# Pair 6 of the output projection by seven products in two of four groups, with its step orders rearranged

## The chip, the core and the metric

The kernel runs on one core of a Trainium2 chip. The core has TensorE (matrix products into PSUM, eight banks of 512 fp32 columns), VectorE, ScalarE and GpSimd (POOL) beside it, and queues that start DMA transfers; SyncE (SP) issues most loads. Each engine executes its own instructions in order and meets the others at semaphores. The metric is the time of one execution in microseconds (us), lower being better; runs are given as a median with the lowest and highest.

## The reference

One layer of a streaming encoder on 256 tokens of width 2048, in float32: a norm, a gated linear attention with four heads in chunks of 64 tokens, its output projection added to the residual, a norm, an MLP with squared ReLU added to the residual, and a final norm. Cut to what matters here:

```python
def _gla_mixer(h, w_in, w_gate_up, b_gate, o_norm, w_out):
    proj = h @ w_in                       # q, k, v, r, g_low
    ...
    _, o = lax.scan(step, s0, (qc, k_dec, vc, chunk_decay))
    o = o * lax.rsqrt(jnp.mean(o * o, axis=-1, keepdims=True) + EPS) * o_norm
    ...
    return (o * jax.nn.silu(r)) @ w_out   # (256, 2048) @ (2048, 2048): the output projection

h = h + _gla_mixer(_rmsnorm(h, gla_norm[j]), ...)
h = h + _sq_relu_mlp(_rmsnorm(h, mlp_norm[i]), mlp_w_up[i], mlp_w_down[i])
return _rmsnorm(h, final_norm)
```

The change lies in the output projection, `(o * silu(r)) @ w_out`.

## The kernel before, in words

**Precision by three products.** Every matrix product is made in a reduced fp32 format (`F32R`): each factor is split into a hi part (a rounded copy, made on ScalarE, L118) and a lo part (the rest, made on VectorE: L131 for weights), and a product is hi x hi + hi x lo + lo x hi, three matmuls on TensorE, each with 128 x 128 stationary values and 256 moving columns. Weights come from memory into a `raw` tile (six of them) and are split into `hi` and `lo` tiles (five of each). SP's loads wait for a free raw tile, the splits for free hi and lo tiles.

**The output projection** runs over four groups of 512 output columns (`out_group(g, ...)`, g from 0 to 3). In each group eight steps run over the contraction, a step being a pair of 128 rows (pair kp of `w_out`, 256 rows); the order of the pairs is the tuple `ORDER`. Both halves of the tokens have one PSUM bank each, started with the residual `h` (`begin_out`, called at step 3 for the next group). At the end of a group `h` is written back from the banks.

A step is done in one of two ways. *Plainly*: two halves of tokens x two halves of rows x two blocks of 256 columns = 8 block products, 24 matmuls. *By sums*: a 2 x 2 block product with seven products (Winograd's form of Strassen's method), 21 matmuls. It needs sums of the weight blocks and sums of the activation blocks (*forms*, eight blocks S3, S2, S1, S4, A12, A11, A22, A21 of 128 columns). For the weights:

- the first sum is made by the load: POOL issues a DMA that adds block 1 of the first half onto block 0 in the raw tile (`accum_op`, L742), behind the two loads of 256 KB each (L741) that replace the plain step's one of 512 KB (L744);
- blocks 1 to 3 are cast and split (768 columns), and the first three products (9 matmuls) run;
- `weight_sums` (L602, L603) makes the others in place on VectorE; they are cast (two casts of 512 columns, L118) and split (L771) into a second pair of hi and lo tiles;
- the last four products (12 matmuls) run behind the next step's products (`pending`).

Two of the seven products' targets are the token banks; the others go to the two banks p16 and p57, one pair for all groups. Behind the group's last step by sums ScalarE copies p16 and p57 out (L777, L778), VectorE combines them (L779 to L782) and adds them to `h` with the token banks (L785).

**The turns.** A product needs its activations with the contraction in the partitions. `turn` transposes four blocks of rows of 128 columns on TensorE (L625) into two spare banks and splits them into hi and lo on ScalarE (L638) and VectorE (L639); for a pair that goes by sums `turn_pair` makes the eight forms instead (copies L614, sums L615, cast L616, split L617). The pairs 0, 1 and 7 (`FORMED`) go by sums in all four groups, twelve steps of 32. The last quarter of the attention's output, pairs 6 and 7 among it, is turned in group 0 behind step 1. In the groups 1 to 3 the finished rows of `h` of the group before are turned behind step 1 for the MLP's up projection, which follows.

**What sets the order.** The program is written in the order above, and a planner lays out each engine's queue from it by its own estimates of times; where the text says `tc.issue_after`, an instruction is kept behind another on its engine. `then_mm` keeps blocks of matmuls in the written order (inside one block they may change places). Casts of weights keep their order among each other; copies, sums and turns may come between.

Of the kernel before, what the change touches and what calls it, by code (L numbers as in the profile page):

```python
# [33 lines left out]
T = 256  # L34
# [12 lines left out]
G = 1024  # L47
# [12 lines left out]
OFF = 48  # L60
# [8 lines left out]
def tile_gla_mlp(ctx, tc, x, xt, cols, w_vg, w_in, w_gate, w_out, w_up, w_down, final_norm, out):  # L69
# [19 lines left out]
    def aux_bank():  # L89
        aux_free.rotate(-1)  # L90
        return psum_bank(aux_free[-1], "aux")
# [151 lines left out]
    g2 = lambda kt: colt[:, KT + kt : KT + kt + 1]  # L243
# [88 lines left out]
    h = const.tile([P, NT, D], F32, name="h")  # L332
# [249 lines left out]
    oth = otl = None  # L582
# [13 lines left out]
    def form_sums(f, tt):  # L596
        tt(f[:, S3], f[:, A21], f[:, A11], ALU.subtract)
        tt(f[:, S2 : S1 + 1], f[:, A22 : A22 + 1].to_broadcast([P, 2, P]), f[:, 0::7], ALU.add)
        tt(f[:, S4], f[:, A12], f[:, S2], ALU.subtract)
# [2 lines left out]
        nc.vector.tensor_tensor(u[:, 2], u[:, 0], u[:, 2], op=ALU.subtract)  # L602
        return nc.vector.tensor_tensor(u[:, 1::2], u[:, 1::2], u[:, 2:3].to_broadcast([P, 2, T]), op=ALU.subtract)  # L603

    FORMED = (0, 1, 7)
    in_forms = lambda a: a.rearrange("p (f s) -> p f s", f=8)
    raw_forms = [in_forms(some[:, 4:6].rearrange("p a b -> p (a b)")), in_forms(mid.tile([P, G], F32, tag="db", name="form"))]

    def turn_pair(kp, bank, gain, to):

        raw_form = raw_forms[kp == 1]
        for i in range(2):
            s = bank[:, i * T : (i + 1) * T].rearrange("p (t s) -> p t s", t=NT)
            nc.scalar.activation(raw_form[:, A12 + 1 - i :: 2], s, AF.Copy, scale=gain(2 * kp + i))  # L614
        form_sums(raw_form, lambda o, x, y, op: nc.vector.tensor_tensor(o, x, y, op=op))  # L615
        nc.scalar.copy(to[0], raw_form)  # L616
        nc.vector.tensor_tensor(to[1], raw_form, to[0].bitcast(F32), op=ALU.subtract)  # L617

    def turn(src, row, gain, q, forms_of=None, banks=None):

        bs = banks or [aux_bank(), aux_bank()]
        for i in range(4):
            kt, b, o = 4 * q + i, bs[i // 2], i % 2 * T
            for t in range(NT):
                newest[0] = nc.tensor.matmul(  # L625
                    b[:, o + t * P : o + (t + 1) * P], src[:, t, kt * P : (kt + 1) * P], ident, is_transpose=True,
                    start=i % 2 == t == 0, stop=i % 2 == t == 1, skip_group_check=True,
                ).ins
        for kp in (2 * q, 2 * q + 1):
            if forms_of and kp in FORMED:  # L630
                turn_pair(kp, bs[kp - 2 * q], gain, forms_of(kp))
                continue
            for kt in (2 * kp, 2 * kp + 1):
                i = kt - 4 * q
                b, o = bs[i // 2], i % 2 * T
                s = b[:, o : o + T].rearrange("p (t s) -> p t s", t=NT)
                dh, dl = row(kt)
                nc.scalar.activation(dh, s, AF.Copy, scale=gain(kt))  # L638
                nc.vector.scalar_tensor_tensor(dl, s, gain(kt), dh.bitcast(F32), op0=ALU.mult, op1=ALU.subtract)  # L639
# [5 lines left out]
    oth, otl = (big.tile([P, KT * T + 192], F32R, tag="B", name="ot" + i) for i in "hl")  # L645
# [4 lines left out]
    def forms_o(kp):  # L650
        if kp < 2:
            return [of_pairs[:, kp, i] for i in range(2)]
        return [a[:, OFF : OFF + G].rearrange("p (f s) -> p f s", f=8) for a in (oth, otl)]

    def place_o(kt):

# [5 lines left out]
    def row_o(kt, t):  # L662
        if kt // 2 in FORMED:
            return [a[:, (A11, A21)[t] - kt % 2] for a in forms_o(kt // 2)]
        o, d = place_o(kt)
        return [a[:, o + t * d : o + t * d + P] for a in (oth, otl)]
# [12 lines left out]
    def begin_out(g):  # L679

        for t in range(NT):
            out_banks[g, t] = bank = psum_bank(out_ids[2 * (g % 2) + t])
            nc.scalar.copy(bank, h[:, t, g * GT : (g + 1) * GT])

    def spare_out(g):
        return [psum_bank(out_ids[2 * (1 - g % 2) + t], "aux") for t in range(NT)]

    side.extend([nothing] * 2 + [lambda: (
        turn(on, turned_o, gain_o, 0, forms_o),
        turn(on, turned_o, gain_o, 1, forms_o, [psum_bank(i, "aux") for i in r_banks[4:]]),  # L690
    )])
    side.extend([nothing] * 7 + [lambda: begin_out(0)])
# [7 lines left out]
    GROUPS = D // GT  # L700
# [86 lines left out]
    def ssq_h(g):  # L787
        for t in range(NT):
            sq = tmp.tile([P, GT], F32, tag="t512", name="sq", bufs=1)
            nc.scalar.activation(sq, h[:, t, g * GT : (g + 1) * GT], AF.Square, accum_out=hs[:, t, g : g + 1])  # L790

    ORDER = (3, 0, 2, 1, 4, 7, 5, 6)
    newest[0] = None
    ordered[0] = True
    out_group(0, ORDER, FORMED, {
        1: lambda: (turn(on, turned_o, gain_o, 2), turn(on, turned_o, gain_o, 3, forms_o, spare_out(0))),
        3: lambda: begin_out(1),
    })
    hth, htl = (big.tile([P, KT, T], F32R, tag="A" + i, name="h" + i, bufs=1) for i in "hl")
    turned_h = lambda kt: [a[:, kt, :].rearrange("p (t s) -> p t s", t=NT) for a in (hth, htl)]  # L800
    for g in range(1, GROUPS):
        out_group(g, ORDER, FORMED, {
            1: lambda: turn(h, turned_h, g2, g - 1), 4: lambda: ssq_h(g - 1),
            **({3: lambda: begin_out(g + 1)} if g + 1 < GROUPS else {}),
        })
    sums = [big.tile([P, 4, T], F32, tag="E" + i, name="sums", bufs=1) for i in "hl"]
# [444 lines left out]
    for t in range(NT):  # L1251
# [19 lines left out]
        for on_act, lo, hi in ((0, 0, 256), (1, 1280, 1536), (0, 256, 768), (1, 1536, 2048), (0, 768, 1280)):  # L1271
            s = hf[:, t, lo:hi]
# [44 lines left out]
```

## Time and profile before

| | |
|---|---|
| median of 3 runs | 1043.96 us (1043.85 to 1045.01) |
| profiled execution | 1043.57 us, its span 1041.6 us |
| granted TensorE clock, mean | 0.998 |
| output projection in the span | 286.9 to 374.5 us |
| TensorE, VectorE, ScalarE, POOL busy | 99%, 83%, 71%, 12% |

The profile is of one execution; its times run from the span's first instruction. PE is TensorE's matmuls, DVE VectorE, ACT ScalarE, SP SyncE. A row of a group of instructions names line, engine, operation, written and read tiles, shapes and count, then busy time, the mean ns of one and the idle time before it with what ended it. A row of the timeline has start, length, instruction and count, and in brackets the idle time before it with what ended it. A row of a stretch has the busy time of each engine in it, with the count of instructions, the granted clock and the share of time in which the DMA engines were busy. Matmuls overlap, so each shows 0.28 us where one begins every 0.11.

### The profile page before, as it was taken

The page shows a single profiled execution, that of the slowest core. Times are in us where ns is not written, and L with a number is a line of the kernel's source. Part 1 is how long each engine was busy: PE and PEld are TensorE (multiplying, and loading weights), DVE is VectorE, ACT ScalarE, POOL GpSimd, SP SyncE. Part 2 cuts the span into 40 slices and gives each one's busy share as a digit, 9 for nine tenths or more (in the row PEclk, how much of TensorE's full clock was granted, in tenths as well). Part 3 has the DMA queues.
Part 4 walks back from the last instruction along what each step waited for, and adds up shares of the span by engine and source line. Part 5 has one row for each costly group of instructions (what it writes and reads, how often), then busy time and mean ns, then how long its engine had stood idle before and what let it go on. Part 6 is the DMA issues. An engine that isn't in the chain of part 4 may idle for free.

```text
span 1041.6 us, 23168 instructions
## 1 busy us (share of the span) xinstructions
PE 1033.5 (99%) x9058; PEld 1033.3 (99%) x9058; DVE 865.3 (83%) x1171; ACT 736.7 (71%) x1088; POOL 119.8 (12%) x163
## 2 busy tenths in 40 slices
PE   9999999999999999999999999999999999999997
PEld 9999999999999999999999999999999999999997
DVE  5768654657499876889999999999999999999887
ACT  6785544546477665677788788778778778878685
POOL 0000000010111101111111121111111111111100
PEclk9999999999999999999999999999999999999999
DMA  9957665655667787678887888888888988888772
GB/s 340 335 167 217 191 199 143 182 145 179 190 186 208 209 262 195 178 210 228 230 248 218 239 232 225 235 240 219 245 232 225 245 230 228 232 234 221 235 239 91
DMA packets 118733, 226.79 MB, mean 218 GB/s; under 512 B 10672, under 2 KB 27184, under 8 KB 118496
## 3 DMA queue, kind: packets, MB, share of 16 engines
q1 hardware_dynamic: 100096, 207.39, 64.1%
q0 software_dynamic: 17856, 16.26, 10.4%
q8 instruction: 71, 1.16, 0.4%
q10 hardware_dynamic: 672, 1.66, 0.4%
q14 instruction: 38, 0.31, 0.1%
HBM read 223.17 MB, written 2.10 MB: 216 GB/s over the span
## 4 chain that ended last, share of the span: by engine, by line
PE 99%; issue 0%; ACT 0%; DVE 0%; POOLq 0%; POOL 0%; DVEq 0%
PE up L865 33%; PE acc L865 28%; PE acc L176 19%; PE acc L723 8%; PE acc L219 6%; PE aux L219 2%; PE aux L176 1%; PE aux L625 1%; PE aux L521 1%; PE aux L252 0%; ACT sqf L1204 0%; PE acc L422 0%; DVE hf L1276 0%; POOLq L1313 0%; POOL rf L356 0%
## 5 line engine op out<-in xcount | busy, mean ns | idle before, releaser
L118 ACT CAST hi<-raw 128x512 fp32r<-128x512 f32 (+4 forms) x634 | 512.1, 834 | 233.8 <-PE acc L176 69.1
L131 DVE TENSOR_TENSOR lo<-raw,hi 128x768 fp32r<-128x768 f32 (+3 forms) x226 | 238.0, 1057 | 97.2 <-ACT hi L118 94.4
L865 PE MATMUL acc<-hi,act 128*128 128x256 f32 x1696 | 247.7, 276 | 0.0
L865 PE MATMUL up<-hh,hi 128*128 128x256 f32 x1024 | 238.7, 276 | 0.0
L865 PE MATMUL up<-hl,hi 128*128 128x256 f32 x1024 | 238.7, 276 | 0.0
L165 DVE TENSOR_TENSOR lo<-raw,hi 128x1024 fp32r<-128x1024 f32 x160 | 194.8, 1220 | 28.1 <-ACT hi L118 26.0
L865 PEld LDWEIGHTS acc<-hi,act 128*128 128x128 f32 x1696 | 217.6, 188 | 0.0
L865 PEld LDWEIGHTS up<-hl,hi 128*128 128x128 f32 x1024 | 192.3, 188 | 0.0
L865 PEld LDWEIGHTS up<-hh,hi 128*128 128x128 f32 x1024 | 192.3, 188 | 0.0
L1075 POOL DMA_DIRECT2D raw<-in_w_down x112 | 97.3, 869 | 516.3 <-DMA raw<-in_w_down 248.2
L1135 DVE TENSOR_TENSOR lo<-raw,hi 128x1024 fp32r<-128x1024 f32 x112 | 136.5, 1219 | 1.1 <-ACT hi L118 1.1
L865 PE MATMUL up<-hh,lo 128*128 128x256 f32 x1024 | 137.0, 276 | 0.0
L865 PE MATMUL acc<-lo,act 128*128 128x256 f32 x848 | 133.8, 276 | 0.0
L865 PEld LDWEIGHTS up<-hh,lo 128*128 128x128 f32 x1024 | 125.7, 188 | 0.0
L865 PEld LDWEIGHTS acc<-lo,act 128*128 128x128 f32 x848 | 113.4, 188 | 0.0
L176 PE MATMUL acc<-hi,xA 128*128 128x256 f32 (+1 forms) x736 | 106.1, 279 | 0.0
L176 PEld LDWEIGHTS acc<-hi,xA 128*128 128x128 f32 x736 | 94.9, 189 | 0.0
L603 DVE TENSOR_TENSOR raw<-raw 128x512 f32<-128x512 f32 x124 | 85.6, 690 | 3.2
L176 PE MATMUL acc<-lo,xA 128*128 128x256 f32 (+1 forms) x368 | 61.3, 278 | 0.0
L602 DVE TENSOR_TENSOR raw<-raw 128x256 f32<-128x256 f32 x124 | 52.5, 423 | 2.9
L176 PEld LDWEIGHTS acc<-lo,xA 128*128 128x128 f32 x368 | 50.8, 188 | 0.0
L219 PE MATMUL acc<-xA,hi 128*128 128x256 f32 x288 | 49.2, 276 | 0.0
(181 smaller groups left out, 1220.4 us busy)
## 6 DMA issues: line engine op xcount, KB each, us to landing
raw<-in_w_up SPq DMA_DIRECT2D x128, 512.0 KB, 4.7
raw<-in_w_down SPq DMA_DIRECT2D x224, 256.0 KB, 4.4
raw<-in_w_in SPq DMA_DIRECT2D x80, 512.0 KB, 3.9
raw<-in_w_down POOLq DMA_DIRECT2D x112, 128.0 KB, 5.1
raw<-in_w_out SPq DMA_DIRECT2D x20, 512.0 KB, 4.7
raw<-in_w_down SPq DMA_DIRECT2D x16, 512.0 KB, 5.6
raw<-in_w_vg SPq DMA_DIRECT2D x14, 520.0 KB, 8.5
raw<-in_w_out SPq DMA_DIRECT2D x24, 256.0 KB, 3.5
```

The costliest lines, as they stand in the source:

```text
L118: last_hi[0] = nc.scalar.copy(to, raw)
L131: last_lo[0] = nc.vector.tensor_tensor(lo[:, s], raw[:, s], hi[:, s].bitcast(F32), op=ALU.subtract)
L165: last_lo[0] = nc.vector.tensor_tensor(to[1], dst, to[0].bitcast(F32), op=ALU.subtract)
L176: nc.tensor.matmul(o[:, m], x, w[:, m], start=first and c == 0, stop=last, skip_group_check=True)
L219: nc.tensor.matmul(o, u[:, i, s], m, start=kt == 0 and n == 0 and j % 2 == 0, stop=kt == KT - 1 and n == 2, skip_group_check=True,)
L521: nc.tensor.matmul(o, kab[:, k[0], c0 + c, k[1] : k[1] + P], q(qt[:, c0 + c]), start=c == 0, stop=c == 1)
L602: nc.vector.tensor_tensor(u[:, 2], u[:, 0], u[:, 2], op=ALU.subtract)
L603: return nc.vector.tensor_tensor(u[:, 1::2], u[:, 1::2], u[:, 2:3].to_broadcast([P, 2, T]), op=ALU.subtract)
L723: newest[0] = nc.tensor.matmul(bank[:, o + d : o + d + T], x, w[:, d : d + T], start=bank in sums_banks and bank.name not in begun, stop=l ...
L865: newest[0] = nc.tensor.matmul(o, x, w, start=first, stop=last, skip_group_check=True).ins
L1075: nc.gpsimd.dma_start(out=raw[:, :T], in_=src[:, 0, T:], accum_op=ALU.add)
L1135: last_lo[0] = nc.vector.tensor_tensor(to[1][:, :G], u, to[0][:, :G].bitcast(F32), op=ALU.subtract)
```

## The change

Pair 6 joins the pairs that go by sums, but only in groups 2 and 3 (fourteen steps by sums in all); in groups 0 and 1 it stays plain and reads its rows out of the forms. Its forms are made in group 0, behind step 1, where it was turned before, and lie where its rows lay. The scratch tile for forms is now chosen by the pair's parity, so pair 7 takes the one that pair 1 had. Groups 2 and 3 take the pairs in another order, 0 first and 6 and 5 last. In group 3 the turn of `h` stands behind step 3 instead of step 1.

```diff
-    FORMED = (0, 1, 7)
+    FORMED = (0, 1, 6, 7)
...
-        raw_form = raw_forms[kp == 1]
+        raw_form = raw_forms[kp % 2]
...
-        return [a[:, OFF : OFF + G].rearrange("p (f s) -> p f s", f=8) for a in (oth, otl)]
+        c = (12 * T + OFF + 128, OFF)[kp - 6]
+        return [in_forms(a[:, c : c + G]) for a in (oth, otl)]
...
-    ORDER = (3, 0, 2, 1, 4, 7, 5, 6)
+    ORDER = (3, 0, 2, 1, 4, 7, 5, 6), (0, 3, 2, 1, 7, 4, 6, 5)
+    summed = lambda g: FORMED if g > 1 else (0, 1, 7)
...
-    out_group(0, ORDER, FORMED, {
+    out_group(0, ORDER[0], summed(0), {
...
-        out_group(g, ORDER, FORMED, {
-            1: lambda: turn(h, turned_h, g2, g - 1), 4: lambda: ssq_h(g - 1),
+        out_group(g, ORDER[g > 1], summed(g), {
+            3 if g == GROUPS - 1 else 1: lambda: turn(h, turned_h, g2, g - 1), 4: lambda: ssq_h(g - 1),
```

## The prediction

> **What bounds the kernel now.** I read the page first (busy shares, the chain that ended last), then the chain in order of time, then the stretches of the four groups of the output projection.
>
> ```profile
> span 1041.6 us, 23168 instructions
> PE 1033.5 (99%) x9058; PEld 1033.3 (99%) x9058; DVE 865.3 (83%) x1171; ACT 736.7 (71%) x1088; POOL 119.8 (12%) x163
> PE 99%; issue 0%; ACT 0%; DVE 0%; POOLq 0%; POOL 0%; DVEq 0%
> ```
> ```profile
> 335.90 20.82 PE acc L723 x183
> ```
> ```profile
> core 0: us, PE busy (x) PEld busy (x) DVE busy (x) ACT busy (x) POOL busy (x), PEclk, DMA share, GB/s
> 286.90:309.40 22.50, 22.50 (x201) 22.50 (x200) 21.12 (x33) 18.07 (x29) 1.95 (x3) 1.00 0.59 176
> 309.40:331.10 21.70, 21.70 (x193) 21.70 (x192) 20.17 (x28) 16.11 (x27) 3.33 (x4) 1.00 0.76 217
> 331.10:352.80 21.70, 21.70 (x193) 21.70 (x192) 19.51 (x28) 15.74 (x26) 2.62 (x3) 1.00 0.75 214
> 352.80:374.50 21.70, 21.70 (x193) 21.70 (x192) 18.70 (x26) 15.05 (x24) 0.00 (x0) 1.00 0.73 225
> ```
>
> TensorE is the chain from end to end, and in none of the four groups (one row each) does it stand idle, at full granted clock. So a matmul less is time less, every wait of TensorE is time more, and anything else counts only where its cover runs out. One matmul is worth 20.82 / 183 = 0.114 us. A group has 5 x 24 + 3 x 21 = 183 of them and the turn's transposes. VectorE is the second: 19.5 of 21.7 us in the third group.
>
> **The matmuls.** A step by sums has 9 + 12 = 21 matmuls, a plain one 24. Pair 6 becomes a step by sums in the third and fourth group: 2 x 3 x 0.114 = 0.68 us less. Nothing else of TensorE's work changes in number: pair 6 in the first two groups reads its plain rows out of the forms, with the same 24.
>
> **What the two steps add on VectorE and ScalarE.** VectorE, a stretch of the fourth group in order of time, columns start, length, instruction:
>
> ```profile
> 354.35 0.95 DVE L131 TENSOR_TENSOR lo<-raw,hi 128x768 fp32r<-128x768 f32 x1
> 355.21 0.69 DVE L785 TENSOR_TENSOR h<-acc,some 128x512 f32<-128x512 f32 x1
> 355.82 0.42 DVE L602 TENSOR_TENSOR raw<-raw 128x256 f32<-128x256 f32 x1
> 356.27 0.69 DVE L603 TENSOR_TENSOR raw<-raw 128x512 f32<-128x512 f32 x1
> 356.88 1.22 DVE L131 TENSOR_TENSOR lo<-raw,hi 128x1024 fp32r<-128x1024 f32 x1
> 358.01 1.22 DVE L771 TENSOR_TENSOR lo<-raw,hi 128x1024 fp32r<-128x1024 f32 x1
> 359.15 0.87 DVE L639 SCALAR_TENSOR_TENSOR hl<-aux,colt,hh 128x256 fp32r<-128x256 f32 x2
> ```
>
> From start to start: 0.86 + 0.45 + 0.61 + 1.14 = 3.06 us for a step by sums, 1.13 for a plain one. So each of the two steps adds 1.93 us: the third group comes to 19.51 + 1.93 = 21.44 us in a stretch of 21.70 - 0.34 = 21.36, full, and the fourth to 20.63. The waits that VectorE has there (2.2 us of the old third group, 3.0 of the fourth) may not close up. Of the fourth's, 1.6 stand in one wait for TensorE to release a buffer, where VectorE is as far ahead as it may be (below); they are no loss. So by the worst count it falls behind by 21.44 + 2.2 - 21.36 = 2.3 us and by 20.63 + 1.4 - 21.36 = 0.7, 3.0 us. What hides that is the lead of the lo parts over their matmuls:
>
> ```profile
> 371.52 2.36 DVE L165 TENSOR_TENSOR lo<-raw,hi 128x1024 fp32r<-128x1024 f32 x2 [1.60 <-PE acc L723]
> ```
> ```profile
> 341.15 1.22 DVE L131 TENSOR_TENSOR lo<-raw,hi 128x1024 fp32r<-128x1024 f32 x1
> ```
> ```profile
> 346.47 0.39 PE L723 MATMUL acc<-lo,oth 128*128 128x256 f32 x2
> ```
>
> Pair 5 in the third group is ready at 342.37 and first read at 346.47: 4.1 us of lead, the smallest I find in these two groups. So the two steps cost nothing on VectorE, with 1.1 us to spare by the worst count; without that cover they would cost the 3.0. ScalarE casts 768 + 1024 columns instead of 1024: about 1 us a step more (a cast of 1024 is 1.05 us in L616's row below) on 15.7 of 21.7: nothing.
>
> **The forms of pair 6** are made in the first group, in the turn behind step 1, beside those of pair 7.
>
> ```profile
> 299.13 1.22 DVE L617 TENSOR_TENSOR otl<-some,oth 128x1024 fp32r<-128x1024 f32 x1
> 302.78 3.22 DVE L131 TENSOR_TENSOR lo<-raw,hi 128x1024 fp32r<-128x1024 f32 x3
> ```
> ```profile
> L616 ACT CAST oth<-some 128x1024 fp32r<-128x1024 f32 x1 | 1.0, 1046 | 0.0
> ```
> ```profile
> L615 DVE TENSOR_TENSOR some<-some 128x128 f32<-128x128 f32 (+1 forms) x6 | 2.0, 328 | 0.0
> L639 DVE SCALAR_TENSOR_TENSOR otl<-aux,colt,oth 128x256 fp32r<-128x256 f32 x10 | 4.4, 477 | 0.0
> ```
> ```profile
> 301.61 0.39 PE L723 MATMUL acc<-hi,oth 128*128 128x256 f32 x2
> 301.83 0.39 PE L723 MATMUL acc<-hi,otl 128*128 128x256 f32 x2
> ...
> 306.71 0.39 PE L723 MATMUL acc<-hi,oth 128*128 128x256 f32 x2
> ```
>
> ScalarE gets 1.05 us more; VectorE 3 x 0.33 + 1.22 less two of 0.48, 1.25 us more. Covers: pair 7's lo form ends at 300.35 and is first read at 301.83, 1.5 us; pair 6's weights end near 304.0 (the first of three) and are read from 306.71, 2.7 us. If pair 6's forms go ahead of pair 7's, 0.2 us of the first cover is left. I take 0; bounds 0 and 0.8 (1.05 + 1.25 one behind the other, less 1.5).
>
> **The wait the new order adds.** All groups share one pair of banks for the sums (p16, p57). Before, the last step by sums was pair 7, at step 5, and a plain step lay between its end and the next group. Now pair 6's second half ends the third group, and the fourth begins with pair 0 by sums, whose first products go to p16. ScalarE must copy p16 in between:
>
> ```profile
> 306.68 0.59 ACT L777 COPY some<-acc 128x512 f32<-128x512 f32 x1 [0.27 <-PE acc L723]
> ```
> ```profile
> 327.01 2.32 ACT L118 CAST hi<-raw 128x1024 fp32r<-128x1024 f32 x3 [1.95 <-PE acc L723]
> 329.24 0.58 ACT L777 COPY some<-acc 128x512 f32<-128x512 f32 x1
> ```
> ```profile
> 327.04 0.28 PE L723 MATMUL acc<-hi,oth 128*128 128x256 f32 x1
> ...
> 328.40 0.39 PE L723 MATMUL acc<-hi,oth 128*128 128x256 f32 x2
> ```
>
> In the first group the copy started 0.03 us before the 12 products were issued out (306.71), and ended at 307.27: a p16 product right behind would have waited 0.56 us. In the second, casts stood ahead: the copy ended at 329.82, 1.42 us after 328.40. So TensorE, with all that is queued behind it, waits 0.56 to 1.42 us once. Six products of pair 0 go to another bank (two of the three, 0.68 us), and within such a block the order by which instructions are issued may differ from the written one: at 301.61 the hi products of two blocks stand first. With these ahead, 0 to 0.74 remain. Bounds 0 and 1.42; I take 0.4, the middle of the second pair of ends: the casts stood ahead of the copy in the second group, and the planner has moved products in the first.
>
> The Trainium skill, "TensorE: Matmul & The Clock Gate", section "Step-by-step: what each phase is for", says that the matmuls stay in program order and only weight loads are pulled ahead. By it the chip itself would fill nothing of this wait, and if the planner doesn't either, the sum would be -0.68 + 1.42 = +0.74 at worst; no row of this trace shows a matmul waiting for ScalarE. The second group's end has no such wait: its last sums are still at step 5, and the copy there (329.82) is over 1.3 us before the third group's first product (331.1).
>
> **The turns.** In the third group the turn still stands behind step 1, now after 9 + 24 + 12 products instead of 24 + 9, so 1.4 us later; its h rows have more cover. In the fourth, h comes later: two copies of 0.58, four adds of 256 columns (0.42 as in L602's row) and two sums of 0.69 stand behind the last products, 4.2 us. The turn moves past the second half of pair 0, pair 2 and pair 1, to 78 products, 8.9 us, into the group, so some 4 us are left. It takes eight transposes on TensorE as before, four ScalarE and four VectorE copies, no DMA. Their rows are first read by the up projection's fifth step, 374.5 + 4 x 24 x 0.114 = 385.4, some 17 us behind. Both at 0. The last h hangs on pair 6's second half, one plain step (2.7 us) later than on pair 7's. What is made of it ended at 381.74 and was read at 386.29:
>
> ```profile
> 381.46 0.28 DVE L820 TENSOR_SCALAR work<-ident,r 128x128 f32<-128x128 f32 x1
> ```
> ```profile
> 386.29 0.60 PE L828 MATMUL row<-work,ones 128*128 128x128 f32 x4
> ```
> Of 4.5 us of cover 1.8 are left: nothing.
>
> **The loads.** Two more halves of 256 KB instead of one of 512, two more accumulations on POOL.
>
> ```profile
> 346.28 0.88 POOL L742 DMA_DIRECT2D raw<-in_w_out x1 [5.21 <-DVE lo L131]
> 351.15 0.88 POOL L742 DMA_DIRECT2D raw<-in_w_out x1 [3.99 <-DMA raw<-in_w_out]
> ```
> ```profile
> 362.34 0.42 DVE L602 TENSOR_TENSOR raw<-raw 128x256 f32<-128x256 f32 x1
> ```
> ```profile
> DMA to landing us min/median/max: 3.4/4.5/6.4
> ```
> Accumulations follow each other 4.9 us apart, four take 19.5 of 21.4 us; pair 7's lands by 357.6 at the slowest and its sum is made at 362.34. I take 0.
>
> **Sum:** -0.68 + 0.4 + 0 + 0 = -0.28 us. The profiled execution is 1043.57 us (span 1041.6 and 1.97 around it); it would be 1043.29. The median of the three runs, 1043.96, is 0.39 above it; predicted is 1043.7.
>
> **Rivals.** A: the wait for p16 costs its whole 1.42 and pair 7's late forms 0.8: -0.68 + 2.22 = +1.54, 1045.5; for it, the casts ahead of the copy; against, six products that could fill it. Still within 0.2%. B, slower: the accumulations of pair 7 (now right behind pair 1) and pair 6 land late, because their raw buffers come free late. The sum of weights waits at the head of VectorE's queue and holds up every lo part behind it. A delay of one accumulation, 4.9 us, eats the lead of 4.1 and leaves 0.8 at each of four places: -0.68 + 3.2 + 0.4, 1046.9. It decides once the landings slip by more than 4.1 us, or VectorE's lag does; for it, the full third group; against, 4.8 us between landing and use. C: the new plan of the queues takes waits away elsewhere: nearly nothing to take, since TensorE waits nowhere here; at most the 0.68, 1043.3.
>
> **Chances.** Forecast 0.66 (C's end in it), A 0.20, B 0.12, a gain that no row shows 0.02. A measurement of this kernel tells 0.2%, 2.1 us, from no change: faster 0.02, same 0.86, slower 0.12. The range goes from the profiled execution with the whole gain, 1043.57 - 0.68 = 1042.9, to A with half of what the slowest run, 1045.01, lies above the median: 1045.5 + 0.5 = 1046.0; B lies outside.
>
> **What would show it.** Right: 180 matmuls in the third and fourth group; one gap of TensorE under 1.5 us between them, behind it the copy of p16; VectorE near 99% in the third group, still ahead of its readers. Wrong: TensorE waiting for lo parts, for pair 7's forms near 302, or VectorE's sums of weights waiting for DMA.

## The result and the profile after

The kernel before takes 1043.99 us (median of 22 runs, 1043.49 to 1045.01), the changed one 1045.66 (22 runs, 1044.86 to 1046.36): a ratio of 1.0015, 95% interval 1.0009 to 1.0021. Forecast was 1043.7, 0.3 us under the kernel before; it became 1.7 us longer instead. That lies within the range given (1042.9 to 1046.0) and under the 0.2% that I took for the limit of a measurement, but with so many runs the sign is sure, and the sum had the other one. The profiled execution took 1045.25 us.

From the page of the changed kernel, span and TensorE:

```profile
span 1043.5 us, 23178 instructions
PE 1033.9 (99%) x9052; PEld 1033.2 (99%) x9052; DVE 868.7 (83%) x1179; ACT 736.9 (71%) x1093; POOL 121.3 (12%) x165
```

Six matmuls fewer, and yet TensorE is busy 0.4 us longer, with the same 99%. The busy share can't show what happened; the chain of waits in order of time can (start, length, line, count of matmuls). Before:

```profile
287.02 3.75 PE acc L723 x33
...
374.67 11.79 PE up L865 x104
...
975.07 3.63 PE acc L865 x32
...
1012.78 15.88 PE acc L176 x140
```

After:

```profile
287.15 3.75 PE acc L724 x33
...
362.56 12.02 PE acc L724 x102
374.57 10.38 PE up L867 x88
...
976.48 3.63 PE acc L867 x32
...
1014.18 15.88 PE acc L176 x140
```

Two lengths are read from these rows for every kernel below. The *stretch* runs from the output projection's first row to the row of 32 matmuls in the down projection: 975.07 - 287.02 = 688.05 us before, 689.33 after, +1.28. The *end* runs from the row of 140 matmuls to the end of the span: 28.8 and 29.3, +0.5. Where the projection starts differs between executions (287.0 to 288.6 in all the profiles; in the latest, e10, the chain of waits holds a load of the program's first weights until 21.6 us); here it makes 0.13. Together 1.9, which is the difference of the spans.

**In the stretch: the spacing.** Before, the up projection's first four steps take 11.79 / 104 = 0.1134 us a matmul; after, 12.02 / 102 and 10.38 / 88 are both 0.118, four per cent more. TensorE's timeline shows where that begins. Before, around the fourth group's turn (columns as in the timelines of VectorE in the prediction; the next row of two matmuls begins 0.227 us behind the last one, or 0.24):

```profile
356.56 1.04 PE L625 MATMUL aux<-ident,h 128*128 128x128 f32 x8
...
358.38 0.40 PE L723 MATMUL acc<-hi,otl 128*128 128x256 f32 x2
358.62 0.40 PE L723 MATMUL acc<-lo,oth 128*128 128x256 f32 x2
358.87 0.39 PE L723 MATMUL acc<-hi,oth 128*128 128x256 f32 x2
359.09 0.39 PE L723 MATMUL acc<-hi,otl 128*128 128x256 f32 x2
```

After the eight transposes the matmuls come 0.12 us apart, for about a dozen; from 358.87 on 0.113. The step in which this ends is pair 2's. After:

```profile
357.70 0.40 PE L724 MATMUL acc<-hi,oth 128*128 128x256 f32 x2
357.94 0.40 PE L724 MATMUL acc<-hi,otl 128*128 128x256 f32 x2
...
359.14 0.39 PE L724 MATMUL acc<-hi,oth 128*128 128x256 f32 x2
359.36 0.39 PE L724 MATMUL acc<-hi,otl 128*128 128x256 f32 x2
...
361.52 1.04 PE L625 MATMUL aux<-ident,h 128*128 128x128 f32 x8
...
362.87 0.28 PE L724 MATMUL acc<-hi,oth 128*128 128x256 f32 x1
362.99 0.28 PE L724 MATMUL acc<-hi,otl 128*128 128x256 f32 x1
...
386.55 0.28 PE L867 MATMUL up<-hl,hi 128*128 128x256 f32 x1
387.63 0.68 PE L830 MATMUL row<-work,ones 128*128 128x128 f32 x4 [0.81 <-DVE work L822]
...
391.13 0.28 PE L867 MATMUL up<-hh,hi 128*128 128x256 f32 x1
391.24 0.28 PE L867 MATMUL up<-hl,hi 128*128 128x256 f32 x1
```

The 0.12 us begin behind the moved turn and do not end: some 206 matmuls, up to 386.66, are that far apart. Only the up projection's sixth step, behind one whose weights lie differently, is back at 0.11. Pair 2, which stood behind the turn before, had gone by (from 357.70) when the turn came. Its own first dozen take 0.12 us each here too, with no turn ahead of them. So the dozen behind each turn in the trace of before does not show what a turn does, since pair 2's step follows every turn of the projection there; the experiments have to part the two.

**In the stretch: the wait.** The row product (387.63 above) waits for VectorE. The matmul after 386.55 was due at 386.66, so TensorE loses 0.97 us (the 0.81 in brackets is counted from the modelled end of the last matmul). How late its operands are is seen on ScalarE and VectorE. ScalarE before and after, the copies of the sums' banks behind the group's last step by sums:

```profile
372.49 0.58 ACT L777 COPY some<-acc 128x512 f32<-128x512 f32 x1
```
```profile
370.05 5.37 ACT L118 CAST hi<-raw 128x512 fp32r<-128x512 f32 x6 [1.25 <-DVE raw L603]
375.32 0.58 ACT L778 COPY some<-acc 128x512 f32<-128x512 f32 x1
```

VectorE, the last rows of h before, and from them to the row product's operands after:

```profile
377.07 0.68 DVE L785 TENSOR_TENSOR h<-acc,some 128x512 f32<-128x512 f32 x1
```
```profile
371.85 5.76 DVE L165 TENSOR_TENSOR lo<-raw,hi 128x1024 fp32r<-128x1024 f32 x5
...
381.88 1.28 DVE L786 TENSOR_TENSOR h<-acc,some 128x512 f32<-128x512 f32 x2
...
386.06 1.23 DVE L165 TENSOR_TENSOR lo<-raw,hi 128x1024 fp32r<-128x1024 f32 x1 [1.08 <-ACT hi L118]
387.20 0.48 DVE L822 TENSOR_SCALAR work<-ident,r 128x128 f32<-128x128 f32 x2
```

The copies begin 2.8 us later, as they should for one step later. But h is done 5.4 us later (383.16 against 377.75), for five lo parts stand in a row ahead of its adds and more between them; and the row product's operands, at 387.68 against 381.74, are 5.9 us later, for they stand behind a lo part that itself waits 1.08 us for its cast.

**What stayed quiet.** VectorE's load of the third and fourth group, by stretches (the columns are those of the stretches in the prediction):

```profile
331.10:352.60 21.50, 21.50 (x192) 21.50 (x190) 19.57 (x27) 14.19 (x26) 3.49 (x4) 1.00 0.66 198
352.60:374.50 21.90, 21.90 (x191) 21.90 (x190) 20.49 (x29) 16.63 (x28) 0.87 (x1) 1.00 0.66 197
```

TensorE waits for no lo part, no form and no weight sum. The granted clock is 1.00 in the slow stretch too. And between the third and the fourth group, TensorE and ScalarE:

```profile
352.60 0.62 PE L724 MATMUL acc<-hi,of 128*128 128x256 f32 x4
...
353.28 0.39 PE L724 MATMUL acc<-hi,oth 128*128 128x256 f32 x2
...
355.43 0.39 PE L724 MATMUL acc<-hi,of 128*128 128x256 f32 x2
355.66 0.28 PE L724 MATMUL acc<-lo,of 128*128 128x256 f32 x1
```
```profile
352.57 0.59 ACT L778 COPY some<-acc 128x512 f32<-128x512 f32 x1 [0.42 <-PE acc L724]
```

The planner put pair 0's six products to the other bank first and most of pair 3's behind them; the three to p16 come at 355.43, long after the copy (353.16).

### The profile page after: what moved, and what is told of

The parts are those of the page before. It is cut to its first block, busy times and chain, and to the rows that moved or that the text cites. A ratio compares the mean times of both kernels' runs of the same rounds, so it can differ in the third digit from the quotient of the medians.

```text
span 1043.5 us, 23178 instructions
## 1 busy us (share of the span) xinstructions
PE 1033.9 (99%) x9052; PEld 1033.2 (99%) x9052; DVE 868.7 (83%) x1179; ACT 736.9 (71%) x1093; POOL 121.3 (12%) x165
## 4 chain that ended last, share of the span: by engine, by line
PE 98%; DMA 0%; issue 0%; ACT 0%; DVE 0%; SPq 0%; POOLq 0%; POOL 0%; DVEq 0%
PE up L867 33%; PE acc L867 28%; PE acc L176 18%; PE acc L724 8%; PE acc L219 6%; PE aux L219 2%; PE aux L176 1%; PE aux L625 1%; PE aux L521 1%; DMA raw<-in_w_vg 0%; ACT hi L118 0%; ACT sqf L1206 0%; SPq L168 0%; DVE lo L165 0%; PE acc L422 0%
```

## The experiments

All differences below are against the kernel before (stretch 688.05, end 28.8), unless said otherwise.

| run | median us | ratio (95%) | stretch | end |
|---|---|---|---|---|
| the changed kernel | 1045.66 | 1.0015 (1.0009 to 1.0021) | +1.28 | 29.3 |
| e1_turn_alone | 1044.77 | 1.0008 (0.9999 to 1.0017) | +0.93 | 28.8 |
| e2_turn_shift_first | 1044.72 | 1.0008 (0.9999 to 1.0017) | +0.58 | 28.8 |
| e5_no_offset | 1047.34 | 1.0034 (1.0022 to 1.0046) | +3.27 | 28.8 |
| e7_thirteen | 1044.70 | 1.0006 (0.9996 to 1.0015) | +0.60 | 28.8 |
| e9_last_turn_later | 1044.73 | 1.0007 (0.9998 to 1.0016) | +0.34 | 29.3 |
| e6_turn_back | 1044.82 | 1.0008 (0.9998 to 1.0017) | +0.66 | 29.2 |
| e3_pair2_behind_turn | 1045.20 | 1.0012 (1.0004 to 1.0021) | +0.91 | 29.3 |
| e4_pair2_pair6_early | 1045.17 | 1.0012 (1.0003 to 1.0021) | +0.91 | 29.3 |
| e8_both_mended | 1043.64 | 0.9997 (0.9988 to 1.0006) | -0.68 | 29.2 |
| e10_loads_halved | 1044.24 | 1.0004 (0.9995 to 1.0013) | 0.00 | 29.2 |
| e11_mended_one_load | 1043.07 | 0.9991 (0.9983 to 1.0000) | -0.68 | 28.9 |

The medians of single kernels move by some tenths with the start of the projection; the stretch is read from one profile each, but where the plan of the projections is the same it repeats to 0.01 us (before and e10, e8 and e11), so it carries the verdicts. By the medians alone most of these kernels can't be told from the one before: only the changed kernel, e5, e3 and e4 have intervals clear of 1.

**The theory.** The moved turn costs about 0.9 us of spacing, since no step with the differing layout follows it; pair 6 at the group's end costs 0.97 at the row product; the six matmuls are saved as said. The rival: the slower spacing comes with the fourteen sums (VectorE and the accumulating loads busier, memory shared), and the place of the turn has no part in it.

### The turn alone, and the layout

The kernel before, with the turn of the fourth group moved and nothing else:

```diff
-            1: lambda: turn(h, turned_h, g2, g - 1), 4: lambda: ssq_h(g - 1),
+            3 if g == GROUPS - 1 else 1: lambda: turn(h, turned_h, g2, g - 1), 4: lambda: ssq_h(g - 1),
```

> The kernel before, with one edit: the fourth group's turn stands behind step 3 instead of step 1, so behind pair 2 instead of ahead of it. Theory R (rhythm): a turn leaves TensorE in a slower rhythm, one matmul of 256 columns every 0.118 us instead of 0.1134, until a step with the shifted row layout has passed (pair 2 in the projection, the fifth step of the up projection). Then some 105 + 104 matmuls between this turn and the last turn run slow: +0.9 to +1.0 us, about 1044.9, with rows 0.12 apart from near 362 to near 388 and no wait. Rival T (traffic): the slower rhythm came from DMA and VectorE traffic, which two more steps by sums brought; here it doesn't come, and the time stays within 0.2 us of before. Rival Q (queues): only waits cost; no change.

The chain, fourth group from the turn on and the up projection's first steps:

```profile
363.36 12.37 PE acc L723 x105
375.73 12.25 PE up L865 x104
```

12.25 instead of 11.79 for the same 104 matmuls, +0.93 us over the stretch, without any of the sums of pair 6. The rival falls: the place of the turn is enough.

Now the other side: the kernel before with pair 2's rows laid like all others, so that no step of the projection has the differing layout (its two rows of blocks stand 64 columns further apart than others, and their two halves of tokens 48; `place_o`). The rows behind pair 2's begin 128 columns earlier with it; pair 3, which runs ahead of the first turn, keeps its 0.113 us:

```diff
-    BOTH = (4, 5)
+    BOTH = (99,)
```

> The kernel before, with pair 2's rows laid like all others (no shift of 64 columns, no gap between the two halves of tokens). Theory R: nothing ends the slower rhythm behind the turn of the first group until the up projection's fifth step: some 33 + 3 x 183 + 183 - 33 + 104 matmuls, about 800, times 0.0045 us, less the twelve slow ones of pair 2 in each group that both have: +3.0 to +3.6 us, about 1047.3. Rival T: the layout has nothing to do with it; within 0.3 us of before.

```profile
293.43 21.56 PE acc L723 x183
```

Each group takes 21.56 instead of 20.82 for its 183, from the first group's turn on, and the first up steps 12.25 for 104: +3.27 us. So a turn starts the slow spacing that lasts, and pair 2's layout ends it. That it is these two is shown; what makes it so is not.

The third run takes e1's kernel and lays the weights of the first up step with a gap between their halves, as the fifth has them:

```diff
-                even = ((4,), (0,))[q] if m == 0 else ...
+                even = ((0, 4), (0,))[q] if m == 0 else ...
```

> The kernel before with the fourth group's turn behind step 3 (the first experiment, +0.93 us), and the up projection's first step too gets the shifted weight layout. Theory R: the slow rhythm ends in that step, some 85 matmuls early: 0.35 to 0.4 us less, +0.55. If the fifth step ends the rhythm for another reason than its layout, +0.93 stays.

```profile
375.30 11.89 PE up L865 x104
```

The up steps are back at 11.89 (0.10 over 11.79, which is some 22 matmuls still slow, nearly the whole first step), 0.35 us of the 0.93 return. So the layout may be that of weights as well as of activations.

### The row product's wait

The changed kernel with the last turn, and the row product ahead of it, one step later in the up projection:

```diff
-    ... + [nothing] * 2 + [last_turn])
+    ... + [nothing] * 4 + [last_turn])
...
-                even = ((4,), (0,))[q] if m == 0 else ...
+                even = ((5,), (0,))[q] if m == 0 else ...
```

> The changed kernel, with the last turn (the row product and the turn of the fourth group's rows) one step of the up projection later, and the step with the shifted weight layout moved along, from the fifth to the sixth. All times are from the projection's first matmul to the down projection, against the kernel before: the changed kernel is +1.28 us. If the row product's wait for VectorE (0.97) is a loss of its own, it goes, and the slow rhythm runs 24 matmuls (0.1 us) longer: +0.4. If the wait only follows from the late end of the fourth group and moves along with the row product, +1.3 stays.

The wait is gone, and the stretch falls from +1.28 to +0.34: 0.94 of the 0.97. What is left is -0.68 and the spacing, now over 24 matmuls more (102 + 128 at 0.0044 us each is 1.01): +0.33.

In the next, pair 6 goes by sums in the third group only:

```diff
-    summed = lambda g: FORMED if g > 1 else (0, 1, 7)
+    summed = lambda g: FORMED if g == 2 else (0, 1, 7)
```

> The changed kernel with pair 6 by sums in the third group alone, thirteen steps; orders and turns as in the changed kernel. The fourth group's last step by sums is then pair 7, at step 4. The row product's wait goes (0.97), three matmuls come back (0.34), the slow rhythm stays: against the kernel before +0.6 to +0.7 us between the projection's first matmul and the down projection. If the wait doesn't hang on pair 6's place at the end, +1.6.

Half the saving (-0.34), the whole spacing (+0.93), no wait: +0.59 worked out, +0.60 measured. So the wait comes with pair 6's sums in the fourth group.

Last, the changed kernel with the turn back behind step 1:

```diff
-            3 if g == GROUPS - 1 else 1: lambda: turn(h, turned_h, g2, g - 1), ...
+            1: lambda: turn(h, turned_h, g2, g - 1), ...
```

> The changed kernel with the turn of the fourth group back behind its first step, and nothing else. By the theory of the rhythm, pair 2 then stands behind the turn again and the 206 slow matmuls (0.118 us each) go: -0.99 us. But the turn would come at about 357.7 on the changed kernel's scale, and the second sum of h that it reads ends at 359.15 there: TensorE waits about 1.4 us or more once. The row product's wait of 0.97 stays. So the stretch of the projections is 1.3 to 1.8 us longer than before (the changed kernel: 1.28), the time 1045.3 to 1046. By my prediction's step, that the moved turn costs nothing in its new place and about what its h is late in the old one, the kernel would be slower than the changed one by the whole 1.4 us: 1047.

```profile
358.01 0.38 PE L625 MATMUL aux<-ident,h 128*128 128x128 f32 x2
359.52 0.88 PE L625 MATMUL aux<-ident,h 128*128 128x128 f32 x6 [1.12 <-DVE h L786]
```

The spacing is cured, and the turn waits for h once: from its first transpose to the matmul behind its last it takes 2.14 us instead of 0.79, so what follows comes 1.35 us late, and -0.68 + 1.35 = +0.67 is the +0.66 measured. That is 0.6 to 1.1 us less than I expected, because the row product's wait, which I had thought would stay, is gone: its operands are ready at 385.81, 1.6 us ahead. Pair 6's sums end the group here too; but VectorE's queue is laid out otherwise, with the adds to h (from 380.85) and the operands each ahead of a lo part that stood ahead of them in the changed kernel. So the wait of 0.97 is not pair 6's lateness alone but its lateness together with the places that the planner chose. And the move of the turn, against leaving it, cost 0.62 us in the stretch (1.28 against 0.66): what it avoided, 1.35, was less than the 0.93 and 0.97 that came with it, the second by way of the plan.

### Pair 2 behind the turn

If the theory holds, an order that leaves the turn late and puts pair 2 behind it should take the 0.93 away. Two such orders of the fourth group in the changed kernel:

```diff
-    ORDER = ..., (0, 3, 2, 1, 7, 4, 6, 5)
+    ORDER = ..., (0, 3, 2, 1, 7, 4, 6, 5), (0, 3, 1, 7, 2, 4, 6, 5)     # e3
+    ORDER = ..., (0, 3, 2, 1, 7, 4, 6, 5), (0, 3, 1, 7, 2, 6, 4, 5)     # e4
...
-        out_group(g, ORDER[g > 1], summed(g), {
+        out_group(g, ORDER[max(g - 1, 0)], summed(g), {
```

> The changed kernel, but the fourth group takes its pairs as 0, 3, 1, 7, 2, 4, 6, 5, so that pair 2 follows the turn behind step 3. The same fourteen steps by sums. Theory R: the slower rhythm ends with pair 2's first twelve matmuls: 0.9 us less than the changed kernel, and the wait of the row product for the last h (1.0 us) stays: about 1044.7. Rival T: as much traffic as in the changed kernel, the rhythm stays slow to the last turn: 1045.6.

> As the run before, and pair 6 is taken at step 5 instead of 6 in the fourth group (0, 3, 1, 7, 2, 6, 4, 5), so that the copies of the sums' banks start one plain step, 2.7 us, earlier. If the rhythm (1.0 us) and the row product's wait (1.0 us) are the two losses, both go and the six matmuls remain: 1043.99 - 0.68, about 1043.3, and TensorE waits for nothing between 287 and 392. If the chain to the last h is held by the up projection's splits in VectorE's queue rather than by pair 6's place, the wait shrinks by less than half: about 1044.1.

Both missed: +0.91. The spacing is cured in both (11.97 for 105, 11.79 for 104 up matmuls) and no row product waits, but a new stall came, ahead of the turn (e4, TensorE and then VectorE):

```profile
359.26 0.50 PE L724 MATMUL acc<-lo,oth 128*128 128x256 f32 x3
359.92 1.54 PE L724 MATMUL acc<-hi,of 128*128 128x256 f32 x8 [0.16 <-ACT hi L118]
361.98 0.74 PE L724 MATMUL acc<-lo,of 128*128 128x256 f32 x4 [0.52 <-DVE lo L772]
```

```profile
358.06 0.68 DVE L786 TENSOR_TENSOR h<-acc,some 128x512 f32<-128x512 f32 x1
...
360.70 1.23 DVE L772 TENSOR_TENSOR lo<-raw,hi 128x1024 fp32r<-128x1024 f32 x1
```

These twelve matmuls are pair 1's second half. In both orders pair 1 comes a plain step earlier than in the changed kernel, behind 0 and 3 alone, while VectorE still adds the third group's banks to h (358.06); its sums of weights are made behind that add, and their lo part begins at 360.70. In the changed kernel that lo part begins at 361.98 and is read at 364.40, and nothing waits. Here the matmul after the three was due at 359.60. By 361.98 eight matmuls go by, 0.91 us of work: 1.47 us lost, 1.59 by the end of the twelve (the turn begins at 362.55). -0.68 + 1.59 = +0.91. So VectorE's cover, which I took for whole, runs out when sums stand this close behind the start of a group. The number of steps by sums in a row does not decide it: the next kernel has three in a row, later in the group.

### Both mended

So an order with one more plain step ahead of pair 1 than the changed kernel has, 0, 3, 4, 2, 1, 7, 6, 5, the turn behind the third step (with pair 2 next), and the last turn later as in e9 (the same two edits as there, not shown again):

```diff
-            3 if g == GROUPS - 1 else 1: lambda: turn(h, turned_h, g2, g - 1), ...
+            2 if g == GROUPS - 1 else 1: lambda: turn(h, turned_h, g2, g - 1), ...
...
-    ORDER = ..., (0, 3, 2, 1, 7, 4, 6, 5)
+    ORDER = ..., (0, 3, 2, 1, 7, 4, 6, 5), (0, 3, 4, 2, 1, 7, 6, 5)
```

> The changed kernel with both losses taken out by order alone: the fourth group takes its pairs as 0, 3, 4, 2, 1, 7, 6, 5 with the turn behind step 2, so that pair 2 follows it and the sums stand late, and the last turn comes one step of the up projection later, as two runs above. If rhythm and row product are the only losses: -0.68 us between the projection's first matmul and the down projection, a median near 1043.3. If the three steps by sums in a row (1, 7, 6) make VectorE late, as the weight sums of pair 1 were when pair 7 stood right behind it and pair 2 did not stand ahead, +0.5 or more.

```profile
361.93 12.65 PE acc L724 x111
374.58 14.51 PE up L867 x128
```

TensorE keeps 12.65 / 111 and 14.51 / 128, 0.114 and 0.113, and waits for nothing in the stretch; the three steps by sums in a row (1, 7, 6) make nothing late. -0.68 us exactly: the whole of what the six matmuls were worth. The median is 0.35 under the kernel before, which this measurement can't tell from none; 0.4 us are lost at the end.

### The end

In the runs so far, the kernels with twelve and thirteen steps by sums end in 28.8 us, all with fourteen in 29.2 to 29.3. The changed kernel has two more transfers on SP's queue. The first run gives the kernel before just these, pair 6's weights in the third and fourth group in two halves, without the sums; the second takes them from the mended kernel and leaves it the sums:

```diff
-            if by:                               # e10, on the kernel before
+            if by or (kp == 6 and g > 1):
                 for i in range(2):
                     last_load[0] = nc.sync.dma_start(out=raw[:, i * GT : (i + 1) * GT], in_=src[:, i])
```
```diff
-            if by:                               # e11, on e8_both_mended
+            if by and kp != 6:
                 for i in range(2):
                     last_load[0] = nc.sync.dma_start(...)
-                nc.gpsimd.dma_start(out=raw[:, :T], in_=src[:, 0, T:], accum_op=ALU.add)
             else:
                 last_load[0] = nc.sync.dma_start(out=raw.rearrange("p (i c) -> p i c", i=2), in_=src)
+            if by:
+                nc.gpsimd.dma_start(out=raw[:, :T], in_=src[:, 0, T:], accum_op=ALU.add)
```

> The kernel before; only the loads of pair 6's weights in the third and fourth group are cut into two halves of 256 KB each (two transfers more, no arithmetic changed). If the longer end of the changed kernel comes from the number of transfers and the semaphores that they take in turn, the end (from TensorE's last row of 140 down-projection matmuls to the end of the span) grows from 28.8 to about 29.3 us and the stretch from the output projection's first matmul to the down projection's stays at 688.05 within 0.05: +0.5 us in the time, about 1044.5. If the end hangs on something else of the change (the accumulating transfers, the fourteen sums), it stays at 28.8 and the time does not move.

> The changed kernel with the fourth group's order and the last turn mended (pair 2 behind the turn, the last turn two steps later), and now pair 6's second half of weights loaded with its first in one transfer of 512 KB in the third and fourth group, so the kernel has as many transfers of this kind as the one before; the fourteen sums stay. By the number of transfers the end comes back from 29.2 to 28.8 us, the stretch of the projections stays 0.68 shorter than before, and the time is about 1043.3, 0.7 under the kernel before. If the end does not hang on that number, it stays at 29.2 and the time is about 1043.7.

SP's last instructions, the views of the program's last line (count, ns, first and last start; SP goes through semaphore instructions and then drains). After, and e11:

```profile
L1315 SPq EVENT_SEMAPHORE  x12: 17/28/28, 1039.2 to 1043.4; - x12
L1315 SPq DRAIN  x3: 7/7/7, 1042.5 to 1042.9; - x3
```
```profile
L1316 SPq EVENT_SEMAPHORE  x12: 17/28/28, 1037.2 to 1041.1; - x12
L1316 SPq DRAIN  x3: 7/7/7, 1040.2 to 1040.5; - x3
```

3.3 us from the first semaphore instruction to the first drain after, and 3.3 in e10; 3.0 in e11, as before. The two transfers alone lengthen the end from 28.8 to 29.2 (e10) with a stretch that is the same to 0.01 us; without them the fourteen steps end in 28.9 (e11). So some 0.3 to 0.4 of the 0.5 us are the two transfers'; 0.1 is not accounted for. It does not grow by the transfer: e7, with one more than before, ends in 28.8. What in the two makes the closing longer stays open.

e11 is also the best version: 1043.07 us (1042.72 to 1043.58), a ratio of 0.9991 (0.9983 to 1.0000), 0.91 under the kernel before and 2.6 under the changed one. The trace shows 0.57 of the 0.91 (0.68 in the stretch, less 0.11 at the end); the rest is not traced to anything, and the interval reaches no change.

## Why the prediction was wrong

**The matmuls: right.** -0.68 us; e8 and e11 show it bare.

**Two more steps on VectorE and ScalarE cost nothing: right for the changed kernel.** It waits for no lo part. The working was too dark for the third group (21.44 us of 21.36 worked out, 19.57 measured) and overlooked where the work went: VectorE's combining of the last group's banks and its adds to h (four of 0.42 and two of 0.64, 3 us), which began at 373.80 before, begin at 377.53 after, where the row product hangs on them. And the cover is thin: with pair 1 one plain step earlier (e3, e4) it is gone, and 1.6 us are lost.

**Pair 6's forms: right.** No wait near 302.

**The wait for p16, 0.4 us: wrong by 0.4.** The row taken was the second group's, with casts ahead of the copy. At the third group's end the copy stood ahead of the casts, began as the last of the twelve products were issued and was done 0.6 us later; and the planner filled not only with the six products of pair 0 but with most of pair 3's too. The bound below was 0, and 0 it is. That order is the planner's and stands in the program, so the rule I had cited (the Trainium skill, "TensorE: Matmul & The Clock Gate", section "Step-by-step: what each phase is for": matmuls stay in program order) isn't touched.

**The turns, "Both at 0": this step failed.** I counted the transposes, the copies, the transfers and the cover of h, which held (of the cover 2.4 us were left where I had worked out 4), and asked what the turn would wait for and who waits for the turn. I did not ask what stands behind it on TensorE. The transposes change the spacing of the matmuls behind them until pair 2's step, and the new order takes the turn past pair 2. The trace of before could not have told how much: the dozen slow matmuls behind each turn there (rows of two with 0.24 instead of 0.227 us from start to start) are pair 2's own, as slow without a turn. But it did show two spacings; I had divided 20.82 by 183 and never looked at the starts. +0.93 us (e1).

**The last h, "Of 4.5 us of cover 1.8 are left: nothing": this step failed.** The term was the 2.7 us of a later step; measured are 5.9. I moved the whole chain (copies, adds, square sums, row operands) as a block, and on in-order queues it is no block: the later start let six casts on ScalarE and five lo parts on VectorE, and more in between, go ahead of it. 1.8 of cover against 3.2 of delay more is a wait of 1.4 by this count, 0.97 in the trace, since TensorE was itself 0.4 later there. e6 shows the other lay of the queue, with none.

**The loads, 0: right for their landing, wrong for the end.** Two transfers more made the program's closing 0.3 to 0.4 us longer.

The sum by what the runs show: -0.68 + 0.93 + 0.97 = +1.22 of +1.28 in the stretch, and 0.5 behind it.

**The rivals.** A gave nearly the time that came (1045.5 against 1045.66) by luck, for none of its mechanism came: neither the p16 wait nor the late forms. B's landings were never late; the kind of stall it described, lo parts held up behind sums of weights, has its like in e3 and e4, where sums of weights and their lo part come late, from a full VectorE and not from the loads. C missed that a new plan can also add waits. "Same" was the likeliest outcome by the bound of 0.2%, and 0.15% it was; the direction was wrong.

## What to carry to other kernels

When an operation is moved on a saturated TensorE, ask not only what it waits for and who waits for it, but what it does to those that follow, up to the next thing that undoes it: read the distance between starts behind it, since a busy share of 99% hides four per cent, and where the trace of before always has the two side by side, as the turn and pair 2's step here, move one of them alone. When a chain on shared in-order queues starts later, do not shift its end by the same amount: list what becomes ready in between and may be queued ahead of it. And where a kernel is full, try a gain together with the order that it needs: here every kernel with only a part of the mending was longer in the stretch, and the mended order gave the whole 0.68 us.

## What the hardware showed that I had not expected

- Behind the transposes of a turn TensorE starts 256-column matmuls every 0.118 us instead of 0.1134 (12.25 and 11.79 us for 104), at a granted clock of 1.00, until a step passes whose activations lie like pair 2's (rows 64 and halves of tokens 48 columns further apart; e1, e5) or whose weights have a gap between their halves (e2). It lasts as long as none comes: through all four groups in e5. Pair 2's own first dozen take 0.12 us each whether a turn stands ahead of it or not (357.70 to 359.14 in the changed kernel). The Trainium skill, "TensorE: Matmul & The Clock Gate", section "Wait — 56ns, not 53.3ns?", puts the spacing at N / 2.4 + 2.5 ns with the clock at full, 109 ns for 256 columns as an estimate. Both spacings here are longer, in a stream where each matmul has a weight load of its own (9058 of each before), and a second spacing at the same clock that section does not mention. The cause of the two stays open.
- Two loads cut into two halves each, more than 650 us ahead of the end of the program, lengthen the end by 0.3 to 0.4 us (e10, e11).
